# Turning the second half of each token tile by DMA instead of TensorE at a transformer trunk's five inner norms

## The chip, the core and the metric

The kernel runs on one NeuronCore of a Trainium2 chip. Its metric is device time in microseconds, from launch to the last byte of the output. The core has TensorE (PE; its weight loads are listed apart as PEld), VectorE (DVE), ScalarE (ACT), GpSimd (POOL) and SyncE (SP), which here issues DMAs. Each engine works through its own list of instructions in order. Engines wait for each other by semaphores only.

## The reference

The trunk has two layers over 256 tokens of width 1024, in float32, with causal attention. Each layer does three residual steps, each closed by a layer norm:

```
x = LN(alpha*x + 0.5*SwiGLU_1(x))
x = LN(alpha*x + Mixer(x))
x = LN(alpha*x + 0.5*SwiGLU_2(x))
```

SwiGLU has 2816 hidden columns. The mixer projects x to seven parts and runs a spatial gating unit and a differential attention with rotary embedding; their gated sum goes through `w_out`. So there are six norms. The last one writes the output. The other five, called inner norms here, hand x to the next matrix product.

## The kernel before

**Numbers.** Each float32 operand of a product is split into a high part (`hi`, `whi`, `lhi`, `x[:, :T]`), rounded by an ACT copy, and a low part (`lo`, `wlo`, `llo`, `x[:, T:]`), which DVE gets by subtracting. A product is three matmuls: hi times hi, lo weight times hi, hi weight times lo (`three`, L268).

**Tokens and layouts.** The 256 tokens are two tiles of 128 rows, t = 0 and t = 1 (`x_tok`, printed as `xtok_143` and `xtok_144`). The residual and its norm are kept with tokens on the partitions. The next product needs x with columns on the partitions, so each normalized tile is turned. The turned x has two halves, h = 0 for columns 0 to 511 and h = 1 for 512 to 1023 (`self.x[h]`, printed as the tile `x`, with a serial number for each half).

**An inner norm** (class `Norm`, L509). Behind a feed-forward step `finish_s` (L547) has ACT take the sum of squares; behind a mixer `finish` (L573) gets both moments from DVE's `BN_STATS`. DVE then takes a reciprocal square root in some eight operations on one column (L236) and writes the normalized rows `y` in two instructions of 512 columns (L555, L580), first columns 0 to 511, then the rest. The generator `turned` (L607) is put aside with two delays, (2, 1.5) for t = 0 and (2, 1) for t = 1, in beats that PE's code counts as it emits matmuls; when a delay is over, `turn` (L620) is emitted, for h = 0 and then h = 1. It has PE do four 128x128 transposing matmuls into a PSUM bank (L624), ACT four scaled and shifted copies to `xf` (L630), then ACT the high part (L233) and DVE the low part (L234) of x.

**The product behind a norm** (`gemm_b2`, L377) runs tile 0 with x's first half, tile 0 with the second, then tile 1 likewise. Its loops emit 12 matmuls for each bank and half, so 24 in a row for each tile and half. Tile 0's two turns lie among the last matmuls of the step before; tile 1's lie among those of tile 0 with the second half. For the first weights `ahead` (L197) or the first loads of `stream` (L155) provide the hi and lo copies.

**Order.** PE's order is that in which the code emits it. For ACT, DVE and SP the framework's scheduler sets a fixed order at build time, by priorities; `soon()` (L119) raises the priority of what is emitted inside. SP issues the weight loads (`raw`, 1 MB, four buffers), each of which waits until DVE has read the buffer's earlier content.

**Transposing transfers** are there already elsewhere. `planes` (L182) has ACT sort the 32-bit words of 512 columns into a plane of low and a plane of high 16-bit halves. `turning` (L186) is a transposing DMA of these from SP, and `join` (L192) has ACT interleave the turned planes to 32-bit words again. The attention uses them with `both` and `tt`, and the feed-forward step a like sequence (L694 to L696, L680) with `planes` and `turned`.

Of the kernel before, what the change touches and what calls it, by code (L numbers as in the profile page):

```python
# [15 lines left out]
U16 = mybir.dt.uint16  # L16
AF = mybir.ActivationFunctionType
# [3 lines left out]
P = 128  # L21
D = 1024
T = 256
NT = T // P
# [34 lines left out]
def trunk(ctx, tc, x, xT, w13a, w13b, w2s, w2p, wb, wqk, wa, wbr, wo, gateb, sgug, sgub, sguwT, sgubias, lam, diffg,  # L59
          lng, lnb, lngT, lnbT, cosT, sinT, out):  # L60
    nc = tc.nc
    V, A, G, PE = nc.vector, nc.scalar, nc.gpsimd, nc.tensor
# [15 lines left out]
    def name(s):  # L78
        serial[0] += 1
        return f"{s}_{serial[0]}"  # L80
# [37 lines left out]
    @contextmanager  # L118
    def soon():  # L119
        was = tc.cur_priority  # L120
        tc.cur_priority = max(0, was - 2 * STEP)
        yield
        tc.cur_priority = was
# [11 lines left out]
    def turn(task):  # L135
        try:
            task[0] = clock[0] + next(task[1])
        except StopIteration:
            tasks.remove(task)

    def beside(task, delay):
        tasks.append([clock[0] + delay, task])
# [8 lines left out]
    def behind(ins):  # L151

        return tc.issue_after(ins) if ins is not None else nullcontext()
# [28 lines left out]
    def planes(pk, src):  # L182

        A.activation(pk.rearrange("p (w k) -> p w k", w=2), src.bitcast(U16).rearrange("p (k w) -> p w k", w=2), AF.Copy)

    def turning(pk, n):  # L186

        tt = slots("tt", 2)[0][:, : n * P].bitcast(U16)
        nc.sync.dma_start_transpose(out=tt.rearrange("p (c t) -> p c t", c=2 * n), in_=pk)
        return tt  # L190

# [40 lines left out]
    def split(hi, lo, src):  # L232
        a = A.activation(hi, src, AF.Copy)  # L233
        return a.ins, V.tensor_tensor(out=lo, in0=src, in1=hi.bitcast(F32), op=ALU.subtract).ins  # L234
# [221 lines left out]
    b = side_bank()  # L456
# [5 lines left out]
    ident = const.tile([P, P], F32, name="ident")  # L462
# [40 lines left out]
    def bc_load(src, after):  # L503
        t = res.tile([P, D], F32, tag="bc", name=name("bc"), bufs=2)
        V.tensor_copy(t[:, :1], after)  # L505
        G.dma_start(t, src.partition_broadcast(P))  # L506
        return t

    class Norm:  # L509
# [5 lines left out]

        def __init__(self, l, i, scale, eps, after, last=False):
            self.scale, self.eps, self.last, self.done = scale, eps, last, set()
            self.ends, self.xlo, self.pre = [None] * NT, {}, None
            self.gT, self.bT = (v[:, l, i] for v in (ln_g, ln_b))
            self.y = x_tok  # L520
            self.group = 256 if last else 512
            self.st = [sm("st", D // self.group * 6, bufs=2) for _ in range(NT)]
            self.g, self.b = bc_load(lng[l, i], after), bc_load(lnb[l, i], after)
            if last:
                A.activation(self.g, self.g, AF.Copy, scale=-0.5)
                self.minus = s512("minus")
                A.activation(self.minus[:, :P], ident, AF.Copy, scale=-1.0)
                self.eps_t = self.minus[:, 2 * P : 2 * P + 1]
                V.memset(self.eps_t, eps)
                with behind(silu[0]):  # L530
                    A.activation(sm("first", 1), mask[:, :1], AF.Sqrt)
            else:
                self.x = [xs.tile([P, 4, 512], F32R, tag="x", name=name("x")) for _ in range(2)]
# [13 lines left out]
        def finish_s(self, t, waits):  # L547
            y, st = self.y[t], self.st[t]
            minus, ss = sm("mv", 1), sm("ss", 1)
            V.tensor_scalar(out=minus, in0=st[:, :1], scalar1=st[:, 1:2], scalar2=-1.0 / D, op0=ALU.add, op1=ALU.mult)  # L550
            with soon():
                A.activation(s512("sq").bitcast(BF16), y, AF.Square, bias=minus, accum_out=ss)
            r = rsqrt(ss, self.eps, 1.0 / D)
            for s in (slice(0, 512), slice(512, D)):
                self.ends[t] = V.tensor_scalar(out=y[:, s], in0=y[:, s], scalar1=minus, scalar2=r,  # L555
                                               op0=ALU.add, op1=ALU.mult).ins
            beside(self.turned(t, waits), 0)

        def part(self, t, c, ps, scale=None):
# [13 lines left out]
        def finish(self, t, waits):  # L573
            y = self.y[t]
            mv = sm("mv", 2)
            V.bn_aggr(out=mv, in_=self.st[t])
            if not self.last:
                r = rsqrt(mv[:, 1:2], self.eps)
                for s in (slice(0, 512), slice(512, D)):
                    self.ends[t] = V.tensor_scalar(out=y[:, s], in0=y[:, s], scalar1=mv[:, 0:1], scalar2=r,  # L580
                                                   op0=ALU.subtract, op1=ALU.mult).ins
                beside(self.turned(t, waits), 0)
                return
            cuts = [slice(*c) for c in ((768, D), (0, 512), (512, 768))]
            ve, sd, r, a = (sm(n, 1) for n in ("ve", "nwy", "nwa", "nwy"))
            G.tensor_scalar(out=ve, in0=mv[:, 1:2], scalar1=self.eps, scalar2=None, op0=ALU.add)
            A.activation(sd, mv[:, 1:2], AF.Sqrt, bias=self.eps_t)
            rows = [y[:, s] for s in cuts]
            if t == NT - 1:
                rows[1:] = [side_bank()[:, : s.stop - s.start] for s in cuts[1:]]  # L590
                for b, s in zip(rows[1:], cuts[1:]):
                    PE.matmul(b, ident, y[:, s], start=True, stop=False)
                diag = self.minus[:, P : 2 * P]
                A.activation(diag, self.minus[:, :P], AF.Copy, scale=mv[:, 0:1])
                for b, s in zip(rows[1:], cuts[1:]):
                    PE.matmul(b, diag, self.g[:, s], start=False, stop=True)
            for s in cuts[: 1 if t == NT - 1 else 3]:
                V.scalar_tensor_tensor(out=y[:, s], in0=y[:, s], scalar=mv[:, 0:1], in1=self.g[:, s],
                                       op0=ALU.subtract, op1=ALU.mult)
            V.reciprocal(out=r, in_=sd)  # L600
            V.tensor_scalar(out=a, in0=r, scalar1=r, scalar2=ve, op0=ALU.mult, op1=ALU.mult)
            V.tensor_scalar(out=r, in0=a, scalar1=3.0, scalar2=r, op0=ALU.subtract, op1=ALU.mult)
            for n, (s, v) in enumerate(zip(cuts, rows)):
                V.scalar_tensor_tensor(out=y[:, s], in0=v, scalar=r, in1=self.b[:, s], op0=ALU.mult, op1=ALU.add)
                (nc.sync, A)[n % 2].dma_start(out[t * P : (t + 1) * P, s], y[:, s])

        def turned(self, t, waits):  # L607
# [5 lines left out]
            with behind(self.xlo[1, 1]):  # L613
                for v, op in ((self.g, ALU.mult), (self.b, ALU.add)):
                    V.tensor_tensor(out=self.y[t], in0=self.y[t], in1=v, op=op)

        def ready(self, t, h):
            assert (t, h) in self.done, (t, h)

        def turn(self, t, h):  # L620
            self.done.add((t, h))
            b = side_bank()
            for k in range(4):
                PE.transpose(b[:, k * P : (k + 1) * P], self.y[t][:, h * 512 + k * P : h * 512 + (k + 1) * P], ident)  # L624
            xf = s512("xf")
            hi, lo = (self.x[h][:, :, o + t * P : o + (t + 1) * P] for o in (0, T))
            with soon(), behind(early[0] if t == 0 else None):
                for k in range(4):
                    s, f = slice(k * P, (k + 1) * P), slice(h * 4 + k, h * 4 + k + 1)
                    A.activation(xf[:, s], b[:, s], AF.Identity, scale=self.gT[:, f], bias=self.bT[:, f])  # L630
                with behind((None, self.ends[1])[h] if t == 0 else None):
                    last = split(hi, lo, xf.rearrange("p (k t) -> p k t", k=4))
            self.xlo[t, h] = last[1]
            if (t, h) == (1, 1):
                latest[:] = last
# [457 lines left out]
```

## Time and profile before

| what | before |
|---|---|
| median of 3 runs (lowest to highest) | 1215.0 us (1214.85 to 1215.0) |
| the profiled execution's own time | 1215.4 us |
| its span, first to last instruction | 1213.7 us |
| PE, PEld, DVE, ACT busy | 1207.2, 1016.2, 950.4, 833.1 us |
| DMA read and write mean | 210 GB/s |
| transposing matmuls at inner norms (L624) | 80, in 20 groups of four |
| transposing transfers | 40 of `turned`, 8 of `tt` |

The inner norms' transposing matmuls lie at 178 to 194 us (feed-forward step to mixer), 422 to 438 (mixer to feed-forward step), 600 to 616 (feed-forward to feed-forward step of the next layer), 779 to 794 and 1023 to 1038. In the rows of a timeline the first column is the start in us, the second the duration of the row (of all its instructions together where it ends in x2 or more), then engine, line, operation, output and input. Instructions on ACT and DVE overlap a little, so the distance from start to start is what one costs its engine. A bracket at the end names idle time ahead and what ended it.

### The profile page before, as it was taken

The numbers are of one execution on the slowest core, as the hardware profiler recorded it, in microseconds if no ns is written. First come the engines' busy times: TensorE is split into PE (matmuls) and PEld (weight loads), VectorE is DVE, ScalarE is ACT, GpSimd is POOL, SyncE is SP. The second block draws the span as 40 slices with busy tenths as digits, with TensorE's granted clock in tenths as the row PEclk, the third lists the DMA queues.
The fourth block names the chain that finished last, engine by engine and source line by source line (L and its number), as shares of the span: only waits on it lengthen the run. The fifth ranks groups of instructions, "written<-read, shape, count | busy, mean of one in ns | idle before, by whom it ended". The sixth has DMA issues, their size and how long they took to land.

```text
span 1213.7 us, 16560 instructions
## 1 busy us (share of the span) xinstructions
PE 1207.2 (99%) x6001; PEld 1016.2 (84%) x6001; DVE 950.4 (78%) x1540; ACT 833.1 (69%) x1356; POOL 91.0 (8%) x184
## 2 busy tenths in 40 slices
PE   9999999999999999999999999999999999999998
PEld 8888888888888888888888888888888888888886
DVE  6658998885686985579985679988857879747797
ACT  6677676689865575776766776667897555667761
POOL 0100000233300000000000000002431000000000
PEclk9999999999999999999999999999999999999999
DMA  8975565655754657666667655665547456567551
GB/s 320 336 247 173 213 238 210 218 179 174 236 213 160 216 187 256 191 200 217 213 227 253 195 176 205 252 227 197 176 157 280 169 174 243 186 231 209 186 196 51
DMA packets 90788, 254.39 MB, mean 210 GB/s; under 512 B 55969, under 2 KB 57041, under 8 KB 64081
## 3 DMA queue, kind: packets, MB, share of 16 engines
q1 hardware_dynamic: 86736, 240.41, 58.6%
q0 software_dynamic: 3536, 12.13, 3.1%
q8 instruction: 47, 0.77, 0.3%
q10 hardware_dynamic: 432, 0.79, 0.2%
q14 instruction: 37, 0.30, 0.1%
HBM read 235.47 MB, written 1.05 MB: 195 GB/s over the span
## 4 chain that ended last, share of the span: by engine, by line
PE 97%; DVE 1%; POOL 1%; DMA 0%; ACT 0%; issue 0%; SPq 0%; DVEq 0%; POOLq 0%; ACTq 0%
PE bank L271 38%; PE sbank L271 26%; PE bank L283 16%; PE bank L290 8%; PE sbank L283 2%; PE bank L446 2%; PE sbank L290 1%; PE sbank L821 1%; PE sbank L624 1%; PE sbank L953 1%; PE sbank L870 0%; DMA xraw<-in_xT 0%; DVE wlo L178 0%; PE sbank L868 0%; PE sbank L855 0%
## 5 line engine op out<-in xcount | busy, mean ns | idle before, releaser
L178 DVE TENSOR_TENSOR wlo<-raw,whi 128x1024 fp32r<-128x1024 f32 (+1 forms) x396 | 436.5, 1123 | 150.5 <-ACT whi L174 117.1
L174 ACT ACTIVATE whi<-raw 128x1024 fp32r<-128x1024 f32 (+1 forms) x396 | 374.3, 972 | 148.8 <-PE bank L271 49.5
L271 PE MATMUL bank<-whi,x 128*128 128x512 f32 x840 | 264.6, 390 | 0.0
L271 PEld LDWEIGHTS bank<-whi,x 128*128 128x128 f32 x840 | 157.7, 188 | 32.6
L271 PE MATMUL bank<-wlo,x 128*128 128x512 f32 x420 | 163.5, 389 | 0.0
L271 PE MATMUL sbank<-whi,x 128*128 128x512 f32 x512 | 158.9, 389 | 0.0
L283 PE MATMUL bank<-x,whi 128*128 128x512 f32 x640 | 156.0, 394 | 0.0
L283 PEld LDWEIGHTS bank<-x,whi 128*128 128x128 f32 x640 | 117.1, 188 | 26.3 <-issue 2.7
L271 PEld LDWEIGHTS sbank<-whi,x 128*128 128x128 f32 x512 | 96.1, 188 | 20.0
L353 ACT ACTIVATE shi<-raw 128x1024 fp32r<-128x1024 f32 (+1 forms) x80 | 73.5, 946 | 51.7 <-DVE raw L368 26.7
L271 PE MATMUL sbank<-wlo,x 128*128 128x512 f32 x256 | 99.6, 389 | 0.0
L355 DVE TENSOR_TENSOR slo<-raw,shi 128x1024 fp32r<-128x1024 f32 (+1 forms) x80 | 85.3, 1086 | 14.4 <-ACT shi L353 13.6
L271 PEld LDWEIGHTS bank<-wlo,x 128*128 128x128 f32 x420 | 78.9, 188 | 15.9
L290 PE MATMUL bank<-x,wlo 128*128 128x256 f32 x640 | 85.8, 285 | 0.0
L290 PEld LDWEIGHTS bank<-x,wlo 128*128 128x128 f32 x640 | 81.6, 191 | 2.2
L291 ACT ACTIVATE r<-bank 128x256 f32<-128x256 f32 x112 | 41.7, 376 | 27.2 <-PE bank L290 27.2
L630 ACT ACTIVATE xf<-sbank,ln_b,ln_g 128x128 f32<-128x128 f32 x80 | 30.0, 456 | 38.6 <-PE sbank L624 38.6
L271 PEld LDWEIGHTS sbank<-wlo,x 128*128 128x128 f32 x256 | 48.0, 188 | 9.9
L271 PE MATMUL sbank<-whi,hhi 128*128 128x512 f32 x144 | 56.3, 391 | 0.0
L271 PE MATMUL sbank<-whi,hlo 128*128 128x512 f32 x144 | 56.1, 389 | 0.0
L271 PE MATMUL sbank<-wlo,hhi 128*128 128x512 f32 x144 | 56.1, 389 | 0.0
L506 POOL DMA_DIRECT2D bc<-in_lng x6 | 3.2, 530 | 700.1 <-DVE bc L505 700.1
(246 smaller groups left out, 1997.9 us busy)
## 6 DMA issues: line engine op xcount, KB each, us to landing
raw<-in_w13b SPq DMA_DIRECT2D x76, 1024.0 KB, 5.5
raw<-in_w2p SPq DMA_DIRECT2D x24, 1024.0 KB, 4.8
raw<-in_wa SPq DMA_DIRECT2D x24, 1024.0 KB, 5.3
raw<-in_w2s SPq DMA_DIRECT2D x20, 1024.0 KB, 4.9
raw<-in_wb SPq DMA_DIRECT2D x16, 1024.0 KB, 5.0
raw<-in_wqk SPq DMA_DIRECT2D x16, 1024.0 KB, 4.9
raw<-in_wbr SPq DMA_DIRECT2D x16, 1024.0 KB, 4.9
raw<-in_w13a SPq DMA_DIRECT2D x8, 1024.0 KB, 4.8
```

The costliest lines, as they stand in the source:

```text
L174: copied = A.activation(h, r, AF.Copy)
L178: V.tensor_tensor(out=w, in0=r, in1=h.bitcast(F32), op=ALU.subtract)
L271: PE.matmul(ps, xx, w, start=start and n == 0, stop=stop and n == 2)
L283: PE.matmul(b[-1], hi[:, k * P : (k + 1) * P], xc(k), start=k == 0, stop=False)
L290: PE.matmul(b[n][:, :T], lo[:, k * P : (k + 1) * P], xc(k)[:, :T], start=False, stop=k == KT - 1)
L291: emptied[0] = A.activation(r[:, s], b[n][:, T:], AF.Copy, scale=scale).ins
L353: A.activation(h, r, AF.Copy)
L355: V.tensor_tensor(out=w, in0=r, in1=h.bitcast(F32), op=ALU.subtract)
L446: PE.matmul(ps[t][m], x[:, j, o + t * P : o + (t + 1) * P], y, start=k0 + j == 0 and o == 0 and y is hi, stop=k0 + j == KT - 1 and y is lo)
L624: PE.transpose(b[:, k * P : (k + 1) * P], self.y[t][:, h * 512 + k * P : h * 512 + (k + 1) * P], ident)
L630: A.activation(xf[:, s], b[:, s], AF.Identity, scale=self.gT[:, f], bias=self.bT[:, f])
L821: PE.matmul(banks[m][:, j * nk : (j + 1) * nk], rows(qT, m, j, t * P, P), rows(kT, m, j, 0, nk), start=True, stop=True)
```

## The change

At each inner norm the rows of y are now written second half first. Right behind that half, `send` has ACT make its 16-bit planes and SP issue a transposing transfer of them into a tile `sent`. When the turn of h = 1 is due, ACT joins the planes into `xf` where PE's four matmuls stood, and scales and shifts `xf` in place. The turn of h = 0, the delays, the split into hi and lo and all other code stay. For five norms of two tiles that takes away 40 of the 80 transposing matmuls, and adds 10 `planes`, 10 transposing transfers and 10 joins.

```diff
-    def turning(pk, n):
+    def turning(pk, n, dst=None):
-        tt = slots("tt", 2)[0][:, : n * P].bitcast(U16)
+        tt = (slots("tt", 2)[0][:, : n * P] if dst is None else dst).bitcast(U16)
         nc.sync.dma_start_transpose(out=tt.rearrange("p (c t) -> p c t", c=2 * n), in_=pk)
         return tt
...
     def finish_s(self, t, waits):
...
-            for s in (slice(0, 512), slice(512, D)):
+            for s in (slice(512, D), slice(0, 512)):
                 self.ends[t] = V.tensor_scalar(out=y[:, s], in0=y[:, s], scalar1=minus, scalar2=r,
                                                op0=ALU.add, op1=ALU.mult).ins
+                if s.start:
+                    self.send(t)
...
     def finish(self, t, waits):
...
-                for s in (slice(0, 512), slice(512, D)):
+                for s in (slice(512, D), slice(0, 512)):
                     self.ends[t] = V.tensor_scalar(out=y[:, s], in0=y[:, s], scalar1=mv[:, 0:1], scalar2=r,
                                                    op0=ALU.subtract, op1=ALU.mult).ins
+                    if s.start:
+                        self.send(t)
...
+        def send(self, t):
+            pk = s512("planes").bitcast(U16)
+            with soon():
+                planes(pk, self.y[t][:, 512:])
+                self.sent[t] = turning(pk, 4, t512("sent"))
...
         def turn(self, t, h):
             self.done.add((t, h))
-            b = side_bank()
-            for k in range(4):
-                PE.transpose(b[:, k * P : (k + 1) * P], self.y[t][:, h * 512 + k * P : h * 512 + (k + 1) * P], ident)
             xf = s512("xf")
+            if h:
+                b = xf
+                with soon():
+                    A.activation(xf.bitcast(U16).rearrange("p (k w) -> p k w", w=2),
+                                 self.sent[t].rearrange("p (w k) -> p k w", w=2), AF.Copy)
+            else:
+                b = side_bank()
+                for k in range(4):
+                    PE.transpose(b[:, k * P : (k + 1) * P], self.y[t][:, k * P : (k + 1) * P], ident)
```

The scheduler answers with another order on ACT, DVE and SP. Lines of the changed kernel are a few higher: the scaled copies are L646, the join L636, the transposing matmuls L641, `finish`'s rows L582. Serial numbers of tiles shift too.

First place: ACT at the norm from the first mixer to the feed-forward step behind it. `lhi` and `whi` are high parts of weights, `x_4152` is x's first half, `x_4153` its second, `xf` the scaled turned tile. Before:

```order
L174 ACTIVATE lhi_4432<-raw_4429 128x512
L174 ACTIVATE whi_4439<-raw_4429 128x512 x2
L174 ACTIVATE whi_4459<-raw_4457 128x512 x2
L174 ACTIVATE whi_4465<-raw_4457 128x512
L630 ACTIVATE xf_4321<-sbank_4316,ln_b,ln_g 128x128 x4
```

On the same engine and at the same place now:

```order
L184 ACTIVATE planes_4285<-xtok_143 128x1024
L174 ACTIVATE lhi_4436<-raw_4433 128x512
L174 ACTIVATE whi_4443<-raw_4433 128x512 x2
L174 ACTIVATE whi_4463<-raw_4461 128x512 x2
L646 ACTIVATE xf_4320<-sbank_4321,ln_b,ln_g 128x128 x4
L636 ACTIVATE xf_4350<-sent_4287 128x1024
L233 ACTIVATE x_4152<-xf_4320 128x4x128
```

The planes, which need the normalized rows, stand ahead of five copies of weights, and the join, which needs the transfer, stands ahead of the high part of x's first half. Both halves of the next weight tile (`whi_4465`, now `whi_4469`) have moved behind that.

Second place: DVE at the same norm, from the low part of x's first half for tile 0 to tile 1's moments. `wlo` are low parts of weights; L566 (now L568) adds tile 1's product to the residual. Before:

```order
L178 TENSOR_TENSOR wlo_4466<-raw_4457,whi_4465 128x512 x2
L234 TENSOR_TENSOR x_4152<-xf_4321,x_4152 128x4x128
L566 SCALAR_TENSOR_TENSOR xtok_144<-xtok_144,bank_4156 128x512
L566 SCALAR_TENSOR_TENSOR xtok_144<-xtok_144,bank_4157 128x512
L569 BN_STATS st_4145<-xtok_144 128x6 x2
L576 BN_AGGR mv_4362<-st_4145 128x2
L241 TENSOR_SCALAR ve_4364<-mv_4362 128x1
```

On DVE at that place now:

```order
L234 TENSOR_TENSOR x_4152<-xf_4320,x_4152 128x4x128
L568 SCALAR_TENSOR_TENSOR xtok_144<-xtok_144,bank_4156 128x512
L568 SCALAR_TENSOR_TENSOR xtok_144<-xtok_144,bank_4157 128x512
L571 BN_STATS st_4145<-xtok_144 128x6 x2
L234 TENSOR_TENSOR x_4153<-xf_4350,x_4153 128x4x128
L578 BN_AGGR mv_4362<-st_4145 128x2
L178 TENSOR_TENSOR wlo_4470<-raw_4461,whi_4469 128x512
L241 TENSOR_SCALAR ve_4364<-mv_4362 128x1
```

The two `wlo` that stood ahead of the low part now stand behind tile 1's moments. From there to tile 1's normalized rows DVE's list holds seven operations of 512 columns (`x_4153` and six `wlo`), where it held five (`x_4153` and four `wlo`).

Third place: ACT at the norm from the first feed-forward step to the first mixer (`x_1207` and `x_1208` are x's halves there), now:

```order
L174 ACTIVATE whi_1788<-raw_1780 128x512
L184 ACTIVATE planes_1636<-xtok_143 128x1024
L174 ACTIVATE whi_1788<-raw_1780 128x512
L174 ACTIVATE whi_1820<-raw_1818 128x512 x2
L174 ACTIVATE whi_1826<-raw_1818 128x512
L646 ACTIVATE xf_1676<-sbank_1677,ln_b,ln_g 128x128 x4
L636 ACTIVATE xf_1706<-sent_1638 128x1024
L233 ACTIVATE x_1207<-xf_1676 128x4x128
```

Before, a single `whi` stood between the scaled copies and the high part of x's first half, and neither planes nor join. Elsewhere DVE's and ACT's order differs at some places of the attention.

More of the change, by code (lines that the diff above doesn't have):

```diff
@@ L517, in __init__ @@
             self.scale, self.eps, self.last, self.done = scale, eps, last, set()
-            self.ends, self.xlo, self.pre = [None] * NT, {}, None
+            self.ends, self.xlo, self.pre, self.sent = [None] * NT, {}, None, {}
             self.gT, self.bT = (v[:, l, i] for v in (ln_g, ln_b))
```

## The prediction

> **What bounds the kernel now.** I read the page's busy times first, then the chain of work that ended last.
>
> ```profile
> PE 1207.2 (99%) x6001; PEld 1016.2 (84%) x6001; DVE 950.4 (78%) x1540; ACT 833.1 (69%) x1356; POOL 91.0 (8%) x184
> ...
> PE 97%; DVE 1%; POOL 1%; DMA 0%; ACT 0%; issue 0%; SPq 0%; DVEq 0%; POOLq 0%; ACTq 0%
> ```
>
> PE is busy for all but 6.5 of 1213.7 us, and the chain is PE for 97%. So work taken off PE shortens the kernel, and other work lengthens it only where PE begins to wait. The waits of PE's weight loads come next (line, what it waits for, us in total, times, longest).
>
> ```profile
> PEld sbank L592 <- DVE xtok L571: 1.8, 1, 1.8
> ...
> PEld sbank L821 <- ACT sbank L878: 0.8, 2, 0.5
> ...
> PEld sbank L624 <- DVE xtok L580: 0.7, 2, 0.3
> ```
>
> The longest, 1.8 us, is at the very end. The last row matters most: at both norms behind a mixer PE already waits 0.3 us for normalized rows (L580) before it can turn them. That place has no slack. The third view is the timeline of each engine at the norms, mixer to feed-forward step (410 to 440 us) and feed-forward step to mixer (174 to 192 us).
>
> **What is removed.** PE at the first mixer norm, before:
>
> ```profile
> 426.28 0.39 PE L271 MATMUL bank<-whi,mlo 128*128 128x512 f32 x1
> 426.51 0.60 PE L624 MATMUL sbank<-ident,xtok 128*128 128x128 f32 x4
> 426.86 0.49 PE L271 MATMUL bank<-lhi,x 128*128 128x512 f32 x1
> 427.18 0.39 PE L271 MATMUL bank<-llo,x 128*128 128x512 f32 x1
> ```
>
> One matmul of 512 columns takes 0.23 us from start to start (426.28 to 426.51). From the transposes' start to the second matmul behind them it is 0.67 us, of which the matmul between would take 0.23. A group of four so costs PE 0.44 us. Ten groups go: 10 x 0.44 = 4.4 us, 0.88 for each norm, provided that x's halves are ready when PE arrives earlier. That is the question at each norm.
>
> **What is added.** Planes and joins are known from elsewhere in this trace, at the same size:
>
> ```profile
> 443.64 1.05 ACT L694 ACTIVATE planes<-silu 128x1024 uint16<-128x1024 uint16 x1
> 444.58 2.95 ACT L174 ACTIVATE whi<-raw 128x1024 fp32r<-128x1024 f32 x3
> ...
> 286.68 1.18 ACT L195 ACTIVATE turned<-tt 128x1024 uint16<-128x1024 uint16 x1
> 287.76 0.27 ACT L878 ACTIVATE sbank<-sbank 128x128 f32<-128x128 f32 x1
> ```
>
> From start to start, planes cost ACT 0.94 us and a join 1.08. The transfer, issued at once when its planes are there, has its landing in the DMA view: between 444 and 446 us, with no load issued shortly before, and between 516 and 518 us, with a load 1.7 us ahead:
>
> ```profile
> DMA to landing us min/median/max: 2.7/2.7/2.7
> DMA to landing us min/median/max: 5.2/5.2/5.2
> ```
>
> I take 2.7, because the last weight load stands more than 5 us ahead of tile 0's planes at both places that I looked at:
>
> ```profile
> 415.13 0.33 SPq L161 DMA_DIRECT2D raw<-in_w13b  x1
> ...
> 422.51 3.22 SPq L161 DMA_DIRECT2D raw<-in_w13b  x2
> ...
> 171.51 0.33 SPq L161 DMA_DIRECT2D raw<-in_wqk  x1
> 182.97 3.47 SPq L161 DMA_DIRECT2D raw<-in_wqk  x2
> ```
>
> SP holds the transfer until the planes exist (420.6 and 177.4 us, below), and the next weight loads stand behind it. They are issued only at 422.51 and 182.97, when DVE has read their buffers, so the transfer holds none of them back. For tile 1, SP's timeline is empty from 434 to 442 us, and the planes are there before that. I put SP's part at nothing.
>
> **The mixer norms (2).** ACT and DVE before:
>
> ```profile
> 422.63 1.50 ACT L630 ACTIVATE xf<-sbank,ln_b,ln_g 128x128 f32<-128x128 f32 x4 [2.53 <-PE sbank L624]
> 424.02 0.64 ACT L174 ACTIVATE whi<-raw 128x512 fp32r<-128x512 f32 x1
> 424.54 0.64 ACT L233 ACTIVATE x<-xf 128x512 fp32r<-128x512 f32 x1
> ```
>
> ```profile
> 419.08 1.00 DVE L580 TENSOR_SCALAR xtok<-xtok,mv,nwy 128x512 f32<-128x512 f32 x2
> ...
> 425.30 0.68 DVE L234 TENSOR_TENSOR x<-xf,x 128x512 fp32r<-128x512 f32 x1
> ...
> 430.46 0.68 DVE L178 TENSOR_TENSOR wlo<-raw,whi 128x512 fp32r<-128x512 f32 x1
> 431.06 0.21 DVE L249 TENSOR_SCALAR nwy<-nwa,nwy 128x1 f32<-128x1 f32 x1
> ...
> 433.29 1.00 DVE L580 TENSOR_SCALAR xtok<-xtok,mv,nwy 128x512 f32<-128x512 f32 x2
> ```
>
> Now step by step, with a copy of weights at 0.52 us of ACT (424.02 to 424.54). y's second half is there at about 419.6, half of the pair of 1.00. Planes take to 420.6, and the five copies behind them 2.6, to 423.2. The scaled copies (422.63 to 424.02: 1.39) end at 424.55. The join stands next; its transfer landed at 420.6 + 2.7 = 423.3, so it isn't held, with 1.25 to spare. It takes to 425.63, where x's high part (first half) starts, 1.09 later than before. The low part follows 0.76 behind, at 426.39, and ends 0.68 later at 427.07. PE, 0.44 earlier by the group that is gone, wants it for its third matmul at about 426.97: a wait of 0.1.
>
> The larger effect is behind this low part. Before, DVE takes 433.29 − 425.30 = 7.99 us from there to tile 1's rows, and it is nearly without idle time there (7.70 of 8.00 us busy, in the row below). Now two `wlo` that stood ahead of the low part stand behind it: 2 x 0.60 (430.46 to 431.06) = 1.2 us more. ACT's join holds DVE back while it has nothing else to do, and then the work that could have filled this is in the way. Tile 1's rows start at 426.39 + 7.99 + 1.2 = 435.58. And PE needs the half that is now written second, at the end of the pair: 436.58. PE's arrival:
>
> ```profile
> 433.58 0.39 PE L271 MATMUL bank<-whi,x 128*128 128x512 f32 x1
> 433.89 0.66 PE L624 MATMUL sbank<-ident,xtok 128*128 128x128 f32 x4
> ```
>
> The slot behind 433.58 is 433.81; less 0.44, plus the wait of 0.1, is 433.47. Before, the transposes started 0.1 behind the end of their half (433.79 to 433.89), so now at 436.68: PE waits 3.2 us, made up of 1.09 (join ahead of the high part), 1.2 (two `wlo`), 0.5 (second half first) and PE's own earlier arrival. Net for a norm: −0.88 + 0.1 + 3.2 − 0.1 (the old wait) = +2.3; two norms +4.6. Nothing else is late at tile 1: its high part stands directly behind the scaled copies, and the join comes after.
>
> **The feed-forward norms (3).**
>
> ```profile
> 175.88 1.00 DVE L555 TENSOR_SCALAR xtok<-xtok,mv,nwy 128x512 f32<-128x512 f32 x2
> ...
> 181.62 0.68 DVE L234 TENSOR_TENSOR x<-xf,x 128x512 fp32r<-128x512 f32 x1
> ...
> 188.68 1.00 DVE L555 TENSOR_SCALAR xtok<-xtok,mv,nwy 128x512 f32<-128x512 f32 x2
> ```
>
> ```profile
> 180.87 0.64 ACT L233 ACTIVATE x<-xf 128x512 fp32r<-128x512 f32 x1
> ...
> 184.87 1.15 ACT L552 ACTIVATE sq<-xtok,mv 128x1024 bf16<-128x1024 f32 x1
> ```
>
> ```profile
> 182.76 0.60 PE L624 MATMUL sbank<-ident,xtok 128*128 128x128 f32 x4
> ...
> 190.05 0.60 PE L624 MATMUL sbank<-ident,xtok 128*128 128x128 f32 x4
> ```
>
> Planes from 176.4 to 177.4, four copies (2.08) to 179.45, scaled copies to 180.84, join to 181.92 (its transfer landed at 180.1, 0.7 to spare). The high part so starts 1.05 later than at 180.87, the low part at 182.67, until 183.35. PE arrives at 182.76, where the removed group stood, and wants the low part two matmuls later, at 183.22: a wait of some 0.2. Tile 1's rows depend on ACT's squares at 184.87, which wait for DVE's sums and not for ACT; ACT is through with the second half's scaling by then. y at 188.68 ends at 189.68, also with its halves exchanged ahead of PE's 190.05 − 0.44 + 0.2 = 189.81. So −0.88 + 0.2 = −0.68 each, three norms −2.0.
>
> **The attention's order.** DVE's and ACT's lists differ at a few places there. The row for L821 has 0.8 us of waiting for ACT's L878, in two places where the order changed. It can go (−0.8) or double (+0.8); I take half of it gone, −0.4, since PE arrives with more weights prepared.
>
> **Sum.** −2.0 + 4.6 − 0.4 = +2.2 us on the profiled execution's 1215.4, 1217.6; the median lies 0.4 below that execution, so 1217.2. A measurement of this kernel can tell 0.2% (2.4 us) from no change: faster is below 1212.6, slower above 1217.4.
>
> **Rivals.**
>
> *PE does not wait for tile 1 at the mixer norms.* Then all five norms gain: 5 x −0.88 + 3 x 0.2 + 2 x 0.1 − 0.2 (the old waits) − 0.4 = −4.2, about 1210.8. It decides where y's first half is there by 433.5, 3.1 us earlier than worked out. For it: a fixed order says nothing of how long the semaphores really hold it. Against it: the row of windows (PE, PEld, DVE, ACT, POOL busy, then granted clock):
>
> ```profile
> 410.00:426.00 16.00, 16.00 (x74) 13.25 (x73) 14.99 (x32) 9.08 (x19) 0.99 (x2) 1.00 0.77 267
> 426.00:434.00 8.00, 8.00 (x38) 6.34 (x38) 7.70 (x20) 3.28 (x8) 0.00 (x0) 1.00 0.44 167
> ```
>
> DVE has 0.3 us of idle time there and seven long operations where it had five. Chance 0.14.
>
> *The clock falls behind the new wait: slower.* The granted clock is 1.00 in both stretches, and PE has no wait over 1.8 us, so no row shows what 3.2 us of idle PE do. If PE ran at half rate behind the wait for as long as the wait was, it would lose 1.6 us, 3.2 at two norms: 1220.4. [...] Chance 0.08. [...]
>
> *The transfer lands late: slower.* At 5.2 us instead of 2.7 the join would start at 182.6 instead of 180.84 at a feed-forward norm (+1.75) and at 425.8 instead of 424.55 at a mixer norm (+1.25), and everything behind it with it: 3 x 1.75 + 2 x 1.25 = +7.75, 1225.0. For it: the DMA view's second row. Against it: no load is in flight at the two places looked at, the spare times are 0.7 and 1.25. Chance 0.08.
>
> **How the numbers follow.** The forecast has 0.70. Its own range is 1214.5 to 1219.5: a mixer wait can be off by 0.6 each, a feed-forward norm by 0.2 each, the attention by 0.8. Its middle lies at the bound of 1217.4, so 0.39 of it counts as the same and 0.31 as slower. Of the first rival 0.13 is faster and 0.01 the same; the other two are slower. Together: faster 0.13, same 0.40, slower 0.47. The range runs from 1211.0 to 1221.0: half of the first rival (0.07), the late landing (0.08) and a little of the clock's case lie outside.
>
> **What would show it.** In the changed kernel's waits, L641 for DVE's L582 with two waits of about 3.2 us, in place of 0.3. PE waiting 0.1 to 0.2 for DVE's x (L234) once at a norm. Tile 1's rows on DVE at about 435.6 instead of 433.3 (less what PE gained ahead). Transfers of `sent` landing after 2.7 us. Transposing matmuls at inner norms x40 instead of x80. ACT's busy time up by about 22 us (ten of 1.05 and ten of 1.18). I am wrong if the mixer norms show no wait of over 1.5 us, or if the feed-forward norms cost time.

## The result: 0.3% slower, and the profile after

| | before | changed |
|---|---|---|
| median (lowest to highest) of 8 runs each | 1214.89 us (1214.47 to 1215.0) | 1218.36 us (1216.75 to 1221.19) |
| ratio, 95% interval | | 1.0029 (1.0018 to 1.004) |
| profiled execution, its span | 1215.4, 1213.7 | 1218.69, 1217.0 |

The kernel became slower by 3.5 us. Its executions also spread over 4.4 us, where those of the kernel before lie within 0.5. The page of the changed kernel, busy times and chain:

```profile
PE 1205.4 (99%) x5961; PEld 1012.6 (83%) x5961; DVE 946.0 (78%) x1540; ACT 852.7 (70%) x1376; POOL 91.4 (8%) x184
...
PE 91%; DVE 5%; ACT 2%; issue 1%; SPq 0%; DMA 0%; POOL 0%; DVEq 0%; ACTq 0%; POOLq 0%
```

40 instructions are gone from PE, and it is busy for 1.8 us less (less than the 4.4 us that were taken off it; 1.6 of the difference comes from matmuls at a granted clock of 0.50, which stand 0.43 us apart from start to start in place of 0.23). ACT is busy for 19.6 us more. The chain has 6% less of PE, and DVE and ACT have come in: there are waits now. The waits of PE's weight loads in the changed kernel (line, what it waits for, us in total, times, longest):

```profile
PEld sbank L641 <- DVE xtok L582: 5.5, 2, 2.8
...
PEld bank L271 <- DVE x L234: 2.7, 5, 0.6
...
PEld bank L271 <- ACT x L233: 0.9, 5, 0.2
```

The first row is the wait for tile 1's rows at the two mixer norms, which was 0.7 in total before. The others are tile 0's x, once at each of the five norms. PE's timeline at the first and at the second mixer norm:

```profile
433.25 0.39 PE L271 MATMUL bank<-whi,x 128*128 128x512 f32 x1
436.00 0.66 PE L641 MATMUL sbank<-ident,xtok 128*128 128x128 f32 x4 [2.36 <-DVE xtok L582]
436.41 0.51 PE L271 MATMUL bank<-whi,x 128*128 128x512 f32 x1
436.73 0.62 PE L271 MATMUL bank<-wlo,x 128*128 128x512 f32 x1
437.14 1.05 PE L271 MATMUL bank<-whi,x 128*128 128x512 f32 x2
438.00 0.63 PE L271 MATMUL bank<-wlo,x 128*128 128x512 f32 x1
...
1038.45 0.66 PE L641 MATMUL sbank<-ident,xtok 128*128 128x128 f32 x4 [2.34 <-DVE xtok L582]
1038.86 0.48 PE L271 MATMUL bank<-whi,x 128*128 128x512 f32 x1
1039.17 0.40 PE L271 MATMUL bank<-wlo,x 128*128 128x512 f32 x1
1039.41 0.63 PE L271 MATMUL bank<-whi,x 128*128 128x512 f32 x2
```

Both waits have the same length. But behind the first, two matmuls that are printed as one row need 0.86 us (437.14 to 438.00), behind the second 0.47 (1039.41 to the next row at 1039.88). The windows of the changed kernel name the reason (busy times of five engines, then the granted clock, DMA share and GB/s):

```profile
434.00:436.00 2.00, 0.01 (x1) 0.01 (x1) 1.83 (x6) 0.48 (x1) 0.00 (x0) 1.00 1.13 389
436.00:438.00 2.00, 2.00 (x9) 1.67 (x10) 0.00 (x0) 1.88 (x5) 0.00 (x0) 0.68 0.88 352
438.00:440.00 2.00, 2.00 (x6) 1.62 (x5) 0.69 (x1) 0.83 (x2) 0.00 (x0) 0.50 0.84 221
440.00:442.00 2.00, 2.00 (x10) 1.55 (x10) 0.00 (x0) 1.66 (x3) 0.00 (x0) 0.97 0.00 0
...
1039.00:1041.00 2.00, 2.00 (x10) 1.64 (x10) 0.00 (x0) 1.85 (x6) 0.00 (x0) 1.00 0.97 394
```

The clock fell to half behind the first wait and stayed there for some 3.4 us (2 x 0.32, 2 x 0.50 and 2 x 0.03 us are missing in the three windows, twice 1.7); behind the second it did not fall (e11 shows why). The time of each execution agrees with its mean granted clock:

| time, us | 1216.75 | 1216.94 | 1217.14 | 1218.31 | 1218.41 | 1218.69 | 1219.83 | 1221.19 |
|---|---|---|---|---|---|---|---|---|
| mean clock | 0.999 | 1.000 | 1.000 | 0.999 | 0.999 | 0.999 | 0.997 | 0.997 |

A stretch of 3.4 us at half rate takes 0.0014 off the mean of 1217 us. So the groups read as no halved clock (some 1217), one (1218.4) and two (1220 to 1221). Only the first column doesn't fit: 0.999 alone doesn't show a halved stretch at a norm. In the profile of e9, for one, it comes from the last 2.40 us, where PE has no work left and the granted clock is 0.62.

**Where the time went.** PE's start of the same matmul in both profiled executions, changed less before, just ahead of and behind each stage:

| stage | offset ahead, us | behind | adds | forecast |
|---|---|---|---|---|
| first feed-forward norm | +0.04 | -0.40 | -0.44 | -0.68 |
| first mixer (attention) | -0.40 | -0.14 | +0.26 | -0.2 |
| first mixer norm | -0.14 | +3.25 | +3.39, of which 1.6 at half rate | +2.3 |
| second feed-forward norm | +3.25 | +2.76 | -0.49 | -0.68 |
| third feed-forward norm | +2.76 | +2.28 | -0.48 | -0.68 |
| second mixer (attention) | +2.28 | +1.53 | -0.75 | -0.2 |
| second mixer norm | +1.53 | +3.33 | +1.80 | +2.3 |

(The 1.6 us are the growth of the offset from 436.00 to 440.37, where PE waits for nothing.) With the clock's part taken off, a mixer norm costs 1.8 us and the sum is +1.7.

ACT and DVE of the changed kernel at the first mixer norm: the join, x's high part, x's low part, tile 1's rows.

```profile
424.52 1.18 ACT L636 ACTIVATE xf<-sent 128x1024 uint16<-128x1024 uint16 x1
425.60 0.62 ACT L233 ACTIVATE x<-xf 128x512 fp32r<-128x512 f32 x1
```

```profile
426.25 0.69 DVE L234 TENSOR_TENSOR x<-xf,x 128x512 fp32r<-128x512 f32 x1 [1.96 <-ACT x L233]
...
434.94 1.00 DVE L582 TENSOR_SCALAR xtok<-xtok,mv,nwy 128x512 f32<-128x512 f32 x2
```

The forecast had 424.55, 425.63, 426.39 and 435.58. DVE stands idle for 1.96 us until the high part behind the join is there, as the bracket says. Then it does, ahead of the rows, the two `wlo` for which it had time there. It gets through them in less than thought: 8.69 us from the low part to the rows, forecast 9.19, before 7.99.

### The profile page after: what moved, and what is told of

It reads as the page before. It is cut to its first block, busy times and chain, and to the rows that moved or that the text cites. A ratio compares the mean times of both kernels' runs of the same rounds, so it can differ in the third digit from the quotient of the medians.

```text
span 1217.0 us, 16530 instructions
## 1 busy us (share of the span) xinstructions
PE 1205.4 (99%) x5961; PEld 1012.6 (83%) x5961; DVE 946.0 (78%) x1540; ACT 852.7 (70%) x1376; POOL 91.4 (8%) x184
## 4 chain that ended last, share of the span: by engine, by line
PE 91%; DVE 5%; ACT 2%; issue 1%; SPq 0%; DMA 0%; POOL 0%; DVEq 0%; ACTq 0%; POOLq 0%
PE bank L271 35%; PE sbank L271 24%; PE bank L283 16%; PE bank L290 8%; PE sbank L283 2%; PE bank L446 2%; PE sbank L290 1%; DVE wlo L178 1%; PE sbank L837 1%; PE sbank L969 1%; ACT pp L847 0%; ACT whi L174 0%; DVE nwa L248 0%; PE sbank L886 0%; DVE x L234 0%
## 5 line engine op out<-in xcount | busy, mean ns | idle before, releaser
L710 ACT ACTIVATE planes<-silu 128x1024 uint16<-128x1024 uint16 x40 | 42.0, 1053 | 7.4 <-DVE silu L709 6.2
```

Of the source, the lines that this page charges most:

```text
L710: A.activation(pk.rearrange("p (w k) -> p w k", w=2), s.bitcast(U16).rearrange("p (k w) -> p w k", w=2), AF.Copy)
```

## The experiments

Each run is compared with the kernel before, executed beside it on the same chip. Its medians there were 1215.06 (e1 to e4), 1214.78 (e5 to e8) and 1214.94 us (e9 to e11).

### e1 and e2: the two kinds of norm apart

```diff
-            for s in (slice(512, D), slice(0, 512)):
+            by = True      # e2: False in finish_s, True in finish
+            for s in (slice(512, D), slice(0, 512)) if by else (slice(0, 512), slice(512, D)):
...
-                if s.start:
+                if s.start and by:
                     self.send(t)
...
-            if h:
+            if h and t in self.sent:
...
```

> The change at the three norms behind a feed-forward step alone; the two behind a mixer stay as before. Theory (the loss lies at the mixer norms, where PE waits 2.4 us for tile 1's rows, and the feed-forward norms gain): PE's time there falls by 0.45 us a norm, as in the changed kernel's timeline (3 x -0.45 = -1.35), the attention's new order gives -0.5 in the two layers together, so about 1213.1 us, 0.9985 of before, and executions agree within 0.5 us. Rival (planes, transfers and joins cost time at every norm, in contention): 1214.9 or more.

Measured: 1214.16 us (1213.5 to 1215.35), ratio 0.9993 (0.9984 to 1.0002). Expected was 1213.1: a miss, and as the interval holds 1, no gain is shown by the time alone.

> The change at the two norms behind a mixer alone. Theory: each costs +1.8 us without the clock (wait of 2.4 us, less what the groups gave), and in some executions 1.6 us more for each wait behind which the clock is halved; so between 1218.5 and 1221.7, the median near 1219.5, with a spread of over 1.5 us between executions. Rival (cost spread over all norms): 1216 to 1217.

Measured: 1219.63 us (1219.47 to 1221.92), ratio 1.004 (1.0028 to 1.0053).

The loss is at the mixer norms, as theory had it. The waits of e2 have it in the row that was forecast:

```profile
PEld sbank L643 <- DVE xtok L584: 5.6, 2, 2.8
```

The feed-forward norms gain less than expected. In e1's profiled execution the first two gave 0.5 each, the third lost 0.4, and the attention's new order cost 0.6 in the two layers together (where the changed kernel gained 0.5). Its ACT, PE and DMA view at the third norm:

```profile
781.64 1.18 ACT L638 ACTIVATE xf<-sent 128x1024 uint16<-128x1024 uint16 x1 [0.98 <-DMA sent<-planes]
```

```profile
783.40 0.50 PE L271 MATMUL bank<-lhi,x 128*128 128x512 f32 x1 [0.82 <-ACT x L233]
```

```profile
DMA to landing us min/median/max: 4.3/4.3/4.3
```

This transfer took 4.3 us where the median is 2.7, the join waited 0.98 for it, and PE 0.82 in turn. The last load had been issued 6 us earlier. So the rival of the late landing comes true at single transfers, not at all of them. SP took 2.18 us to issue this one. In the changed kernel's profile nine of the ten took 1.24 to 1.26 and one took 2.11 (landed after 3.5); the late one of e10 took 1.24. What delays them was not found.

### e3: DVE's queue ahead of the rows

```diff
-                    after[3] = [norm.ends[1] if norm.pre else norm.xlo.get((0, 1))] * 2
+                    after[3] = [norm.ends[1]] * 2
```

> The changed kernel, with the four low parts of weights that DVE makes ahead of tile 1's rows at a mixer norm put behind these rows (4 x 0.6 = 2.4 us of DVE). The join stays where it is. Theory (DVE's queue ahead of the rows makes the wait): the rows come 2.4 us earlier, PE waits 0.1 to 0.3 us in place of 2.4, no clock is halved, each mixer norm gains about 0.4: 1214.9 - 1.35 - 0.8 - 0.5 = about 1212.2, executions within 0.5 us. Rival (the wait is the transfer's or the join's, not DVE's queue): PE still waits 1.5 us or more, 1216 or more.

Measured: 1212.68 us (1212.45 to 1213.38), ratio 0.9981 (0.9972 to 0.999). The waits of e3, and PE at the first mixer norm:

```profile
PEld sbank L641 <- DVE xtok L582: 1.8, 2, 0.9
```

```profile
433.38 0.66 PE L641 MATMUL sbank<-ident,xtok 128*128 128x128 f32 x4 [0.47 <-DVE xtok L582]
```

PE now waits 0.5 in place of 2.4 (expected 0.1 to 0.3), the mean granted clock is 0.999 or 1.000 in all eleven executions, which agree within 0.9 us, and the change gains. The transfers and joins are all still there, so it was the queue ahead of the rows that cost the time.

### e4: does waiting alone halve the clock?

Nothing of the kernel's work is in this one: bursts of matmuls, and between them a chain of DVE operations that PE waits for.

```diff
+    for rep in range(8):
+        for n in (4, 0, 6, 2, 7, 1, 5, 3):
...
+            for q in range(m):
+                PE.matmul(b, gate, w, start=q == 0, stop=q == m - 1)
...
+            for _ in range(n):
+                V.tensor_tensor(out=g, in0=src, in1=src, op=ALU.mult)
```

> Leaves the whole computation out (it copies x to the output): 64 bursts of 40 to 50 matmuls of 512 columns, between which PE waits for a chain of 0 to 7 DVE operations, so for some 1 to 5 us, with no transfer in flight. Theory (an idle PE alone halves the clock, from a wait of about 2.4 us on, by where the wait falls): no burst behind a wait under 1.7 us starts slow, part of those behind 2 to 3 us do, all behind more than 3.5 us do; a slow start costs 1.5 to 2 us. [...] Rival 2 (the slow clock came from the transfers or the load around the wait): none at all.

The first three waits with the bursts behind them on PE's timeline, and windows right behind the first and the third wait:

```profile
20.39 12.26 PE L81 MATMUL bank<-w,next 128*128 128x512 f32 x47 [3.55 <-DVE next L87]
33.29 10.08 PE L81 MATMUL bank<-w,next 128*128 128x512 f32 x43 [0.64 <-DVE next L87]
48.38 14.24 PE L81 MATMUL bank<-w,next 128*128 128x512 f32 x50 [5.00 <-DVE next L87]
```

```profile
20.00:24.00 4.00, 3.61 (x10) 2.90 (x11) 0.30 (x2) 0.00 (x0) 0.00 (x0) 0.60 0.00 0
...
48.00:52.00 4.00, 3.62 (x9) 2.85 (x10) 0.29 (x1) 0.00 (x0) 0.00 (x0) 0.50 0.00 0
```

Without a halved clock a burst's row should last 0.227 us for each matmul, and 0.16 more for the tail of the last (the kernel before, at a clock of 1.00: nine matmuls of 512 columns from 739.72 to 741.76, and 0.39 for a row of one). For 47 that is 10.8, and the row has 12.26: 1.4 us lost. For the 43 behind the short wait it is 9.9, and the row has 10.08: nothing lost to speak of. For the 50 behind the longest it is 11.5, and the row has 14.24: 2.7 us lost. No DMA runs in either window. Counted over all 63 waits with a burst behind them (over 1 us lost counts as halved; nothing lies between 0.2 and 1.4):

| wait, us | 0.7 | 1.46 | 2.19 | 2.91 | 3.6 | 4.37 to 5.8 |
|---|---|---|---|---|---|---|
| halved, of | 0 of 8 | 0 of 8 | 3 of 8 | 5 of 7 | 7 of 8 | 24 of 24 |

The clock was halved behind 39 of the 63 waits though nothing of the kernel's work ran beside them, so an idle PE alone did it here, and rival 2 falls. Behind the waits of 2.2 and 2.9 us it was halved in 8 of 15. A halved clock cost 1.5 to 1.7 us behind waits of under 3 us and 1.4 to 2.9 behind longer ones.

### e11: the clock, in finer steps

e4's kernel with other lengths of the chain.

> Leaves the whole computation out (copies x to the output): 112 bursts of 40 to 50 matmuls, with waits of about 1.45, 1.7, 1.95, 2.2, 2.45, 2.7, 2.95 and 3.2 us between them, 14 of each. Theory A (the clock is halved when one free-running window of about 1.7 us passes wholly idle, so with a chance of (wait - 1.7) / 1.7): 0, 0, 2, 4, 6, 8, 10, 12 of 14. Theory B (half of a window of 3.4 us idle is enough): 0 at 1.45, then 7 of 14 at once at 1.7 and about 8 to 12 from 1.95 to 2.95. Theory C (a fixed length of wait, without a window): a step from 0 to 14 between two neighbours.

| wait, us | 1.46 | 1.81 | 2.01 | 2.19 | 2.54 | 2.74 | 2.92 | 3.26 |
|---|---|---|---|---|---|---|---|---|
| halved, of | 0 of 14 | 1 of 14 | 8 of 14 | 5 of 14 | 10 of 14 | 6 of 13 | 12 of 14 | 13 of 14 |

(Three waits of the first round were 0.1 shorter than their column says.) A, B and C are guesses of the author. B is out at 1.81, and C has no step to point to. A has the foot (nothing up to 1.5, one at 1.8) and the end (13 at 3.26), but 8 at 2.01 where it has under 3. The counts alone leave the rule open.

The traces of e4 and e11 settle more than the counts. In their records of the granted clock it changed only at the lines of a grid of 3.413 us that can be laid through the whole execution: the 94 halved stretches behind waits began at such a line and lasted for one window between lines (63 of them) or for two (31). So A's window of 1.7 us is out too. What tells the waits of these two runs apart is how long PE stood idle within a single window. Here a wait is counted from where the matmul behind the last one could have started, some 0.16 us more than in the brackets. For each of the 174 waits take the longest part of it that lies in one window. Where that is under 1.9 us (65 waits) the clock was never halved. Between 1.9 and 2.1 us it was in 3 of 18, and above 2.1 us in 91 of 91. That is nearest to B, with some 2.0 of 3.41 us in place of half.

The changed kernel's two waits of 2.5 us fit it. These are the windows of its grid at the two mixer norms:

```profile
433.31:436.72 3.41, 1.05 (x7) 0.69 (x6) 2.52 (x8) 1.09 (x2) 0.00 (x0) 1.00 0.99 360
436.72:440.14 3.42, 3.42 (x10) 2.65 (x9) 0.69 (x1) 2.11 (x5) 0.00 (x0) 0.50 0.87 283
1034.06:1037.47 3.41, 2.04 (x10) 1.34 (x8) 3.30 (x11) 0.00 (x0) 0.00 (x0) 1.00 0.77 245
1037.47:1040.88 3.41, 2.43 (x13) 2.08 (x14) 0.92 (x2) 2.77 (x6) 0.00 (x0) 1.00 0.99 358
```

The first wait lies in one window as a whole, and the next window has a clock of 0.50. The second is cut by a line of the grid into 1.5 and 1.0 us, and the clock stays. The mixer norms' waits in the profiles of e2, e7 and e8 fit as well: the four with 2.06 to 2.14 us in one window halved the clock, those with 1.75 and 2.01 did not. So in these profiles it was the place of the wait on the grid that decided. That this place differs from one execution to the next would explain how the same kernel comes to spread, but it is a guess: each kernel has the profile of one execution. Why the limit is at 2.0 us, no run here shows.

### e10: the same wait, filled with matmuls

```diff
+                if t == 1 and not self.pre:
+                    for n in range(8):
+                        PE.matmul(b.rearrange("p (k t) -> p k t", k=4), self.x[0][:, 0, :P], self.x[0][:, :, :P],
+                                  start=n == 0, stop=n == 7)
                 for k in range(4):
                     PE.transpose(
```

> The changed kernel with 8 matmuls more on PE ahead of tile 1's transposes at the two mixer norms, whose result is overwritten; they run while PE would wait for the rows (8 x 0.23 = 1.8 of the 2.5 us). The lists of the other engines stay. Theory (the idle wait halves the clock, and that makes the spread): the wait falls under 1 us, the clock stays at 1.00, all executions lie within 0.7 us of the lowest of the changed kernel's, median 1216.9. Rival (the slow stretch comes from what the other engines or the transfers do there): executions spread from 1216.8 to 1221 as before, or the filler costs its 1.8 us each: 1220.

Measured: 1217.12 us (1216.54 to 1218.41), ratio 1.002 (1.0011 to 1.0029). PE and the windows of e10 at the first mixer norm:

```profile
432.70 1.98 PE L642 MATMUL sbank<-x 128*128 128x512 f32 x8
435.22 0.66 PE L645 MATMUL sbank<-ident,xtok 128*128 128x128 f32 x4 [0.55 <-DVE xtok L582]
```

```profile
434.00:436.00 2.00, 1.46 (x9) 0.95 (x9) 1.13 (x3) 1.14 (x2) 0.00 (x0) 1.00 1.00 320
436.00:438.00 2.00, 2.00 (x10) 1.64 (x9) 0.00 (x0) 1.97 (x5) 0.00 (x0) 1.00 0.97 373
```

Sixteen useless matmuls made the changed kernel's median 1.2 us lower. The intervals of the two ratios overlap by a little, but the spans and clocks of the single executions tell them apart: all ten of e10 have spans of 1214.8 to 1216.4 us at a mean clock of 0.999 or 1.000. The changed kernel has 1215.0 to 1215.4 in three executions and 1216.6 to 1219.5 in five. DVE, ACT and the transfers do the same work around these windows, some 0.8 us earlier, and the clock stays at 1.00. So here the idle time halved it, not what goes on beside it. The spread is larger than the 0.7 expected. Two executions were 1.2 us longer outside the core's span, and in the profiled one a feed-forward norm has a transfer that landed after 4.2 us, for which PE waited 0.73.

### e8: tile 0 alone at the mixer norms

```diff
+                by = t == 0     # in finish; finish_s: False; the rest as in e1 and e2
```

> Only tile 0 at the two mixer norms goes by transfer; tile 1 there, and the feed-forward norms, as before (tile 1's rows first half first). Theory: the wait for tile 1's rows comes from tile 0's join and the two low parts behind it, so it stays, less 0.5 for the order of the halves: about 1.9 us at each, and the kernel is about 3 us slower than before. Rival (the wait is tile 1's own transfer or the exchanged halves): wait of 0.5 us or less, 1215.5 or less.

Measured, in a single execution: 1221.91 us. Its waits, and PE at the first mixer norm:

```profile
PEld sbank L643 <- DVE xtok L584: 4.6, 2, 2.3
```

```profile
435.72 0.66 PE L643 MATMUL sbank<-ident,xtok 128*128 128x128 f32 x4 [1.90 <-DVE xtok L584]
```

The wait for tile 1's rows is there although tile 1 itself is as before, 0.46 shorter (1.90 for 2.36), which is the exchanged halves. So tile 0's part of the change makes it: its join ahead of the high part, and the two `wlo` behind. This run does not tell these two apart. The clock fell behind both waits in this execution, and the two halved stretches of some 1.6 us each come on top of the 3 us expected.

### e7: the join one place later

```diff
-                with soon():
+                with soon(), behind(self.hi0 if t == 0 else None):
                     A.activation(xf.bitcast(U16)
...
+            if h == 0:
+                self.hi0 = last[0]
```

> The changed kernel with tile 0's join put behind the high part of x's first half, and nothing else; one of the two low parts that had moved stands ahead of x's low part again. Theory: tile 1's rows at a mixer norm come about 0.9 us earlier (0.56 on ACT, 0.35 on DVE), PE waits about 1.5 there instead of 2.4, too short for the clock; the tile 0 waits of about 0.4 at the feed-forward norms go. 1216.9 (the changed kernel without a halved clock) - 2 x 0.9 - 3 x 0.4 = about 1213.9. Rival (the join's place does not matter, the two moved low parts do): 1216 or more.

Measured: 1219.24 us (1218.69 to 1219.97), ratio 1.0037 (1.0023 to 1.0051). Expected was 1213.9: a miss, by two things. The scheduler filled the join's place with a `whi` on ACT and put one `wlo` ahead of the low part, so the rows came only 0.4 us earlier against PE's arrival:

```profile
436.44 0.76 PE L641 MATMUL sbank<-ident,xtok 128*128 128x128 f32 x4 [1.98 <-DVE xtok L582]
...
PEld sbank L839 <- ACT aT L875: 2.4, 2, 1.5
```

(A timeline row, and one of the waits.) With a wait of 2.0 left the clock still fell at one norm. And the second row is new: in the attention PE waits up to 1.5 us for ACT's copies of the turned attention weights (L875), because ACT's order there came out another way, some 85 us behind the edit. By the offsets the attention now costs 1.5 and 0.8 us in the two layers, where it was +0.3 and -0.8 in the changed kernel. So the time is where the rival had it, but for another reason. What did go is tile 0's wait at the feed-forward norms, which now gain 0.7 each, and a mixer norm costs 1.1 without the clock in place of 1.8. The join's place matters, then; how the rest divides between it and the `wlo` was not tested apart.

### e5, e6, e9: what can be had

e5 puts e3, e7 and first-half-first for tile 1 together.

> The changed kernel with three edits: the four low parts behind tile 1's rows (as in e3), tile 0's join behind the high part of x's first half, and tile 1's rows first half first. Theory: PE's waits at the norms (0.6 at tile 1 of a mixer norm and about 0.4 at tile 0 of every norm in e3) go nearly all, so each norm gives close to its 0.88: 1212.7 - 2 x 0.6 - 5 x 0.35 = about 1210 us, 0.9955 to 0.997 of before, executions within 0.7 us. Rival (the waits at tile 0 come from the transfer or from ACT's planes ahead, not from the join's place): 1211.5 or more.

Measured: 1212.27 us (1211.31 to 1213.36), ratio 0.9979 (0.997 to 0.9988). Expected was about 1210: a miss, and the time lies above the rival's 1211.5. But by the offsets of PE's start in its profiled execution each norm gives 1.0 to 1.1, 5.2 together, a little more than the 0.88 of the working, so the waits at tile 0 did go with the join's place. The attention's order of e7 came along and took 2.2 of it; its row of waits is the same:

```profile
PEld sbank L839 <- ACT aT L875: 2.4, 2, 1.5
```

e6 is e3's line in the kernel before.

> The kernel before, with only e3's edit (four low parts behind tile 1's rows at the mixer norms), no transfers. Theory: nothing to gain but the old waits of 0.3 us, so within 0.5 us of before; e3's gain is then the removed matmuls', not the edit's. Rival (the edit alone gains what e3 gained): 1212.7.

Measured: 1214.77 us (1214.2 to 1215.19), ratio 0.9998 (0.9989 to 1.0007). The line alone gains nothing, so e3's gain comes with the transfers. By the offsets 1.7 us of it lie at the norms, and 0.5 in the attention's order, which is chance.

e9 is e3 with the old order of the halves for tile 1 at the mixer norms; ACT's order in the attention stays.

```diff
-                for s in (slice(512, D), slice(0, 512)):
+                for s in ((slice(512, D), slice(0, 512)) if t == 0 else (slice(0, 512), slice(512, D))):
```

> e3 with one edit more: at the mixer norms tile 1's rows are written first half first again (tile 0's stay second half first). ACT's order in the attention stays that of e3. Theory: PE's wait of 0.6 us for these rows, one half of 0.5 us, goes at both norms: 1212.7 - 1.0 = 1211.7. Rival (tile 1's transfer, now 0.5 us later, is the next thing late): 1212.5 or more.

Measured: 1211.96 us (1211.22 to 1212.79), ratio 0.9975 (0.9965 to 0.9984). It beats both kernels, by 3.0 us and by some 6, and its wait is nearly that of before:

```profile
PEld sbank L641 <- DVE xtok L582: 0.9, 2, 0.4
```

## Why the prediction was right, and where it was off

It forecast 1217.2 us, within 1211.0 to 1221.0, with slower the likeliest. The time is 1218.4. That the two are so close is in part luck: together the mixer norms were put 1.0 too high and the feed-forward norms 0.6 too low, and the clock's 1.6 was left out.

- **What bounds it.** PE, with no slack at the mixer norms' second tile. Right: that is the place where the time was lost (e2).
- **What is removed.** 0.44 us a group. Right: at tile 1 of the first feed-forward norm, where PE waits for nothing, the offset falls by 0.45.
- **The mixer norms.** The mechanism was right: the join ahead of the high part, two `wlo` behind it, the half written second (e3, e8, e9). PE's arrival (433.48) and the delay by the join (x's low part 0.95 later, on a stage 0.14 earlier: 1.09) came as worked out. The wait was put at 3.2 and was 2.5, from 433.48 to 436.00; the bracket's 2.36 counts from the end of the row before. The term that was mis-sized is the two `wlo`: 1.2 in the forecast, 0.7 in the trace. So +1.8 without the clock instead of +2.3.
- **The feed-forward norms.** -0.68 forecast, -0.44 to -0.49 measured. The wait at tile 0 was put at 0.2 and is nearly 0.4 (PE could have started at 183.24 and started at 183.59). PE and DVE of the changed kernel:

```profile
183.01 0.40 PE L271 MATMUL bank<-llo,x 128*128 128x512 f32 x1
183.59 0.73 PE L271 MATMUL bank<-lhi,x 128*128 128x512 f32 x2 [0.19 <-DVE x L234]
```

```profile
182.25 0.68 DVE L178 TENSOR_TENSOR wlo<-raw,whi 128x512 fp32r<-128x512 f32 x1
182.86 0.68 DVE L234 TENSOR_TENSOR x<-xf,x 128x512 fp32r<-128x512 f32 x1
```

  The low part did not start when its high part was there (182.67 by the working) but when DVE was done with a `wlo` that stood ahead of it, at 182.86. And PE went on 0.05 behind its end, which the working left out.
- **The attention's order.** -0.4 forecast, -0.5 measured (+0.26 and -0.75). That it fits is luck: in e5 and e7 the first layer gave +1.5.
- **The late landing.** Its chance was 0.08. It happened at single transfers (4.3 in e1, 4.2 in e10, with 0.7 to 0.8 us of PE each), not at all of them as the rival had it.
- **The clock.** This is the step that failed. The price was right (1.6 us forecast at each wait, 1.6 measured), though it was reckoned as half rate for as long as a wait of 3.2 us, and the changed kernel's trace has a granted clock of 0.50 for 3.41 us behind a wait of 2.5. The chance was not: 0.08 was the author's guess, with no row of the trace before on such a wait, and five of eight executions, by their times, have at least one such stretch. It makes the difference between 1217.2 and 1218.4. The waits were even shorter than forecast and still enough. In e4 and e11 the clock was halved behind 63 of 112 waits of 1.8 to 3.3 us, and behind none of 30 up to 1.5. A step on which the trace before had no row should not have been given so small a chance.

## What to carry to other kernels

Where one engine bounds the kernel, work moved off it is worth its time only as far as the consumer's operands come earlier too. Look at the list of the engine that takes the work: what is put ahead of the critical operation there, and what work is left to stand behind it when it could have filled the gap. And price a new wait of the matrix engine with a second cost, the half clock that may follow it: 1.6 us at the changed kernel's first mixer norm, and in e4 and e11 behind 63 of 112 waits of 1.8 to 3.3 us and none of 30 up to 1.5.

## What the runs showed that had not been expected

- In e4 and e11 the clock was halved for one or two windows of 3.41 us, a loss of 1.5 to 1.7 us mostly, behind waits from 1.8 us on; in e11 the share rose to 13 of 14 at 3.3 us. It went with some 2.0 us of idle PE within one window of the grid (none of 65 waits with under 1.9, all of 91 with more than 2.1). The changed kernel had it in five of eight executions, by their times, so it shows as spread too.
- Eight matmuls whose result is thrown away, put into a wait of 2.5 us at two places, lowered the median by 1.2 us (e10).
- A one-column operation on DVE cost 0.06 us between long ones and 0.19 in a chain. In the changed kernel at the first mixer norm (start, us):

```profile
417.07 0.15 DVE L244 TENSOR_SCALAR yi<-ve 128x1 int32<-128x1 int32 x1
417.26 0.27 DVE L248 TENSOR_SCALAR nwa<-yi,ve 128x1 f32<-128x1 f32 x1
...
430.52 0.15 DVE L241 TENSOR_SCALAR ve<-mv 128x1 f32<-128x1 f32 x1
430.58 0.68 DVE L178 TENSOR_TENSOR wlo<-raw,whi 128x512 fp32r<-128x512 f32 x1
```

  From its start to the next one's it took 0.06 us between the long ones (430.52 to 430.58), and in a chain, where the next needs its result, 0.19 (417.07 to 417.26). With 0.2 us less of idle time (0.30 us on the way before, 0.11 now), that is why two more `wlo` lengthened the way to the rows by 0.7 and not by 1.2.
- A transposing transfer of 256 KB landed after 2.7 us in the median of the changed kernel's ten, but three of these took 3.5, 3.6 and 5.0 us, and single ones took 4.3 in e1 and 4.2 in e10 with no load issued in the 6 us before.
